# Elementwise work off GpSimd in a planned diffusion-transformer block: subtractions, products and fills on VectorE alone, casts on ScalarE without a handicap

## The chip, the cores and the metric

One NeuronCore of a Trainium2 chip runs the kernel. Its engines work side by side, each through its own queue in order: TensorE (PE in the rows; PEld are its weight loads), VectorE (DVE), ScalarE (ACT), GpSimd (POOL) and SyncE (SP, whose queue SPq issues all DMAs here). The metric is the device time of one execution in microseconds. TensorE's granted clock has two levels, 1.2 and 2.4 GHz; the rows show it as a share of 2.4 GHz.

## The reference

Two layers of a latent diffusion block, on 256 latent tokens and 256 context tokens of width 1024. Cut to what matters:

```
for l in range(DEPTH):                                # DEPTH = 2
    mod_x = silu(c) @ w_ada[l] + b_ada[l]             # shift, scale, gate; the same for the context
    hx = rms_norm(x, norm_w[l]) * (1 + scale_x) + shift_x
    px = split(hx @ w_in[l], SPLIT_POINTS)            # q, k, v and gate columns of four mixers
    ...
    qa = rope(rms_norm(px[0]) * gain)                 # all q and k: norm, gain, and rope in A, C, D
    y_a = window_sink_attention(...)                  # B: 2-D neighbourhood, C: dense, D: differential
    ...
    branches = [y_a * silu(px[3]), y_b * silu(px[7]), y_c * silu(px[11]), y_d * silu(px[15])]
    x_new = x + gate_x * (sum_n(sigmoid(g_n) * (branches[n] @ w_br[l, n])) @ w_out[l])
    if l < DEPTH - 1:                                 # the context stream too, in the first layer
        ctx = ...
```

All matrices are float32, and the result is wanted near float32 precision.

## The kernel before

Every large product is made of three matmuls in the fp32r format (`mm3`): an operand is split into a high part, which is the value cast to fp32r, and a low part, the value less its high part. So each weight block `raw` that a DMA brings becomes `wh` (a cast, by ScalarE or VectorE, list `AV`) and `wl` (a subtraction, by VectorE or GpSimd, list `VG`), in `split_ops`. The normalized, modulated input becomes `hT` in an upper half `hh` (a cast) and a lower half `hl` (a subtraction) in `modulate`. The other instructions of list `VG` are the products of q and k with gains, rope tables and inverse norms (tiles `qk`, `ru`, `st`), the bias with its mask, the zeroes beside mixer B's scores, y times its gate, the merge of the four branches (`merged`) and the sums into the residual.

The start is special. Shift and scale (`mods`) of layer 0 come out of 16 units of w_ada, two for each k tile of 128 rows. A unit is made on VectorE (`ada_unit`: two long products with a sum each), on TensorE (`ada_unit_pe`) or by GpSimd and ScalarE (`ada_unit_pool`: GpSimd makes two products of 1024 columns, tiles `t4k` and `V`, and ScalarE sums each). The string `ADA` says which; five units are GpSimd's, and neither version touches that. The first two groups of projections go k tile by k tile behind the units: `mods`, then `t2k` = x * scale + shift, then `hh`, then `hl`, then the matmuls into `ppj`, `psc` and `ptr` that read hT.

The program is first recorded: each call becomes an operation with the engines that may run it, its cost on each and its dependencies (`alt`, `cost`). Then a planner (`schedule`) puts the operations in an order, engine by engine, by a list-scheduling pass over a model of the engines; an operation of several engines goes to the one where it would end first, with `BIAS` added in the comparison. `search` repeats the pass six times with the operations ordered by their latest start and keeps the best. The instructions are then issued in that order, and each engine keeps it. `ready` holds the model's rule that some instructions of VectorE and GpSimd exclude each other (`port`). All instructions go through one helper, so that every row of the profile has the line L271, and tiles tell them apart.

Of the kernel before, what the change touches and what calls it, by code (L numbers as in the profile page):

```python
# [93 lines left out]
TAIL = 2  # L94
HOLD = 12
WARM = 9
AV, VG = ("scalar", "vector"), ("vector", "gpsimd")
BIAS = {"vector": 0.55, "gpsimd": 0.0, "scalar": 0.35}
ENGS = ("tensor", "scalar", "vector", "gpsimd", "sync")
DMA_FIX, DMA_RATE, LOOK = (0.63, 0.93), 360e3, 60  # L100
GATE = 4096 / 1200.0
# [72 lines left out]
class Recorder:  # L174
# [143 lines left out]
    def schedule(self):  # L318
        ops = self.ops
        for o in ops:  # L320
            o.need, o.fin, o.users = len(o.deps), None, []
        for o in ops:
            for d in o.deps:
                ops[d].users.append(o.i)

        first, left = {}, {}
        for name, a in self.acc.items():
            first[name] = min(o.i for o, _, _ in a)
            left[name] = len({o.i for o, _, _ in a})
        fifo, free, index, kind = {}, {}, {}, {}  # L330
        for name in sorted(first, key=first.get):
            tag, bufs = self.tag[name]
            g = GROUP.get(tag, tag)
            kind[name] = g, tag
            q = fifo.setdefault(tag, [])
            index[name] = len(q)
            q.append(name)
            free.setdefault(g, [(0.0, k) for k in range(bufs if g == tag else BANKS)])
        ptr, held = dict.fromkeys(fifo, 0), dict.fromkeys(fifo, 0)
        shared = {g: [d for d in SURE if GROUP[d] == g] for g in set(GROUP.values())}  # L340
        got, since, tend, taken = {}, {}, {}, []
        bank = {}
        avail = {e: [] for e in ENGS}

        def slot_time(o):

            t, used = 0.0, {}
            for name in o.tiles:
                if name in got:
                    t = max(t, since[name])  # L350
                    continue
                g, tag = kind[name]
                k = used.get(tag, 0)
                room = len(free[g])
                if g in shared:
                    room = min(room, max(SURE[tag] - held[tag],
                                         room - sum(max(0, SURE[d] - held[d]) for d in shared[g] if d != tag)))
                ahead = index[name] - ptr[tag] - k
                if room <= k + (RESERVE.get(tag, 99) if ahead > 0 else 0) or ahead > WINDOW:
                    return None  # L360
                t = max(t, sorted(free[g])[k][0])
                used[tag] = k + 1
            return t

        port = dict.fromkeys(ENGS, 0.0)

        def ready(o, e, s):
            r = max(o.at[e], s)
            if o.port[e]:
                r = max(r, port["gpsimd" if e == "vector" else "vector"])  # L370
            for name in o.banks:
                for f, x in bank.get(name, {}).items():
                    if f != e:
                        r = max(r, x + LAT[f, e])
            return r

        def release(o):
            for e in o.ways:
                bisect.insort(avail[e], (o.prio, o.i))
                o.at[e] = max([0.0, o.hold] + [ops[d].fin + LAT[ops[d].eng, e] for d in o.deps])  # L380

        for o in ops:
            o.at = {}
            o.hold = o.late - HOLD if "sync" in o.ways and not o.raw else 0.0
            if o.need == 0:
                release(o)
        t_free = dict.fromkeys(ENGS, 0.0)
        t_free["sync"] = 0.55
        dma_free, order = 0.0, []
        queue = deque(o.i for o in ops if o.raw)  # L390
        work, gate, slow = {}, 0, True
        while len(order) < len(ops):
            best = None
            for e in ENGS:
                tf, c = t_free[e], None
                if best is not None and tf >= best[0]:
                    continue
                for prio, i in (avail[e][:LOOK] if e != "sync" else avail[e]):
                    if ops[i].raw and i != queue[0]:
                        continue  # L400
                    s = slot_time(ops[i])
                    if s is None:
                        continue
                    o = ops[i]
                    s = s + 0.15 if s else 0.0
                    r = ready(o, e, s)
                    if len(o.ways) > 1:
                        mine = max(r, tf) + o.costs[e] + BIAS[e]
                        if any(max(ready(o, f, s), t_free[f]) + o.costs[f] + BIAS[f] < mine
                               for f in o.ways if f != e):  # L410
                            continue
                    if r <= tf:
                        c = (tf, e, i)
                        break
                    if c is None or r < c[0]:
                        c = (r, e, i)
                if c is not None and (best is None or c[0] < best[0]):
                    best = c
            if best is None:
                raise RuntimeError("no instruction can be scheduled")  # L420
            t, e, i = best
            o = ops[i]
            for f in o.ways:
                avail[f].remove((o.prio, i))
            o.eng = e
            if o.raw:
                queue.popleft()
            order.append(i)
            for name in o.tiles:
                if name not in got:  # L430
                    g, tag = kind[name]
                    z = min(free[g])
                    free[g].remove(z)
                    since[name], got[name] = z
                    held[tag] += 1
                    taken.append(name)
                    q = fifo[tag]
                    while ptr[tag] < len(q) and q[ptr[tag]] in got:
                        ptr[tag] += 1
            c = o.costs[e]  # L440
            if e == "tensor":
                while gate < int(t / GATE):
                    slow = work.get(gate, 0.0) < (0.6 if slow else 0.38) * GATE
                    gate += 1
                c *= 1 + slow
                for k in range(gate, int((t + c) / GATE) + 1):
                    work[k] = work.get(k, 0.0) + min(t + c, (k + 1) * GATE) - max(t, k * GATE)
            o.fin = t_free[e] = t + c
            if o.port[e]:
                port[e] = o.fin  # L450
            if o.dma:
                dma_free = max(dma_free, o.fin + DMA_FIX[0]) + o.dma / DMA_RATE
                o.fin = dma_free + DMA_FIX[1]
            o.start = t
            for name in o.banks:
                bank.setdefault(name, {})[e] = o.fin
            for name in o.tiles:
                left[name] -= 1
                tend[name] = max(tend.get(name, 0.0), o.fin)
                if left[name] == 0:  # L460
                    g, tag = kind[name]
                    free[g].append((tend[name], got[name]))
                    held[tag] -= 1
            for u in o.users:
                q = ops[u]
                q.need -= 1
                if q.need == 0:
                    release(q)
        self.makespan = max(o.fin for o in ops)
        self.got, self.taken, self.kind, self.order = got, taken, kind, order  # L470
# [1311 lines left out]
```

## Time and profile before

| | |
|---|---|
| median of three runs | 1323.66 us (1319.93 to 1325.12) |
| the profiled execution | 1319.68 us |
| its span, first to last instruction | 1317.9 us |
| TensorE busy | 1243.6 us, 94% |
| VectorE busy | 1003.8 us, 76% |
| ScalarE busy | 757.1 us, 57% |
| GpSimd busy | 626.9 us, 48% |

The profile is of one execution. A line of a group gives an engine, an operation, the tiles that it writes and reads, the shapes and the count, then busy time and mean duration, then the time that the engine sat idle before it and what ended that. A busy engine is one whose instruction is under way, which includes an instruction that waits inside its engine for a resource.

### The profile page before, as it was taken

How to read it: one execution, taken by the hardware profiler on the slowest of the kernel's cores; microseconds unless marked ns; L12 is line 12 of the kernel's file. 1: busy time of each engine (PE TensorE's matmuls, PEld its weight loads, DVE VectorE, ACT ScalarE, POOL GpSimd, SP SyncE). 2: the span in 40 equal slices, each digit the busy share in tenths (PEclk: the TensorE clock that was granted, in tenths of full speed). 3: DMA queues.
4: the chain of work that ended last, by engine and by line, in shares of the span. 5: the costliest groups of instructions: out<-in, count | busy, mean ns of one | idle time of the engine just before them, and what ended most of it. 6: DMA issues, size and time to landing. Idle time of an engine off the chain costs nothing. (4 is left out here: it accounts for less than half of the span.)

```text
span 1317.9 us, 21363 instructions
## 1 busy us (share of the span) xinstructions
PE 1243.6 (94%) x7286; PEld 1083.4 (82%) x7286; DVE 1003.8 (76%) x2074; ACT 757.1 (57%) x1761; POOL 626.9 (48%) x705
## 2 busy tenths in 40 slices
PE   7379999999999999999999999889999899999998
PEld 5267888888988989888887888788899899998997
DVE  7858983992889587995878667788794767897876
ACT  5356862473775336653555445577784657665663
POOL 4557311623654535512444003474866577574632
PEclk8689999999999999999999999999999899999999
DMA  6532122522343353333322247342434544343554
GB/s 241 159 116 71 49 90 86 160 64 67 103 108 116 108 151 94 91 114 123 115 81 65 80 153 256 94 137 73 152 109 120 177 143 152 122 144 97 155 167 174
DMA packets 64576, 160.90 MB, mean 122 GB/s; under 512 B 13482, under 2 KB 24914, under 8 KB 64468
## 3 DMA queue, kind: packets, MB, share of 16 engines
q1 hardware_dynamic: 64468, 159.55, 39.3%
q8 instruction: 57, 0.93, 0.3%
q14 instruction: 51, 0.42, 0.1%
HBM read 157.42 MB, written 5.88 MB: 124 GB/s over the span
## 5 line engine op out<-in xcount | busy, mean ns | idle before, releaser
L271 PE MATMUL ppj<-wh,hT 128*128 128x512 f32 (+2 forms) x1424 | 387.4, 350 | 34.6 <-ACT hT L271 34.2
L271 ACT ACTIVATE wh<-raw 128x512 fp32r<-128x512 f32 (+2 forms) x432 | 254.6, 603 | 270.5 <-PE ppj L271 196.7
L271 POOL TENSOR_TENSOR wl<-raw,wh 128x512 fp32r<-128x512 f32 (+2 forms) x190 | 221.1, 1172 | 311.6 <-PE ppj L271 164.3
L271 PE MATMUL ppj<-hT,wh 128*128 128x512 f32 (+1 forms) x1408 | 363.3, 342 | 0.0
L271 PEld LDWEIGHTS ppj<-wh,hT 128*128 128x128 f32 x1424 | 253.0, 191 | 60.2 <-ACT hT L271 35.1
L271 DVE TENSOR_TENSOR wl<-raw,wh 128x512 fp32r<-128x512 f32 (+1 forms) x290 | 210.7, 739 | 86.7 <-PE ppj L271 59.7
L271 PEld LDWEIGHTS ppj<-hT,wh 128*128 128x128 f32 x1408 | 241.4, 189 | 26.8 <-PE ppj L271 0.2
L271 PE MATMUL ppj<-wl,hT 128*128 128x512 f32 (+2 forms) x712 | 247.8, 350 | 1.6 <-POOL wl L271 1.6
L271 PE MATMUL ppj<-hT,wl 128*128 128x512 f32 (+1 forms) x704 | 241.1, 343 | 0.4 <-DVE wl L271 0.3
L271 ACT ACTIVATE P<-psc,st 128x512 f32<-128x512 f32 (+2 forms) x192 | 114.7, 601 | 58.8 <-DVE st L271 53.4
L271 PEld LDWEIGHTS ppj<-wl,hT 128*128 128x128 f32 x712 | 136.1, 192 | 13.9 <-POOL wl L271 2.2
L271 PEld LDWEIGHTS ppj<-hT,wl 128*128 128x128 f32 x704 | 133.0, 189 | 14.7 <-DVE wl L271 0.7
L271 PE MATMUL ppj<-yT,wh 128*128 128x512 f32 (+1 forms) x512 | 130.2, 339 | 0.3 <-ACT yT L271 0.3
L271 DVE TENSOR_REDUCE st<-psc 128x1 f32<-128x512 f32 (+2 forms) x160 | 101.2, 661 | 0.8
L271 PE MATMUL psc<-K,Q 128*128 128x512 f32 (+2 forms) x384 | 95.3, 357 | 5.6 <-ACT P L271 2.0
L271 PE MATMUL ptr<-ident,P 128*128 128x128 f32 x560 | 89.7, 277 | 11.5 <-DVE P L271 6.1
L271 POOL TENSOR_TENSOR st<-st,expo 128x8 f32<-128x8 f32 (+3 forms) x68 | 96.2, 1418 | 3.6
L271 PEld LDWEIGHTS ppj<-yT,wh 128*128 128x128 f32 x512 | 87.1, 188 | 10.8 <-ACT yT L271 0.5
L271 PEld LDWEIGHTS ptr<-ident,P 128*128 128x128 f32 x560 | 67.2, 142 | 27.6 <-ACT P L271 8.4
L271 POOL TENSOR_TENSOR ru<-qk,rtab 128x256 f32<-128x256 f32 (+1 forms) x34 | 25.0, 735 | 134.8 <-ACT qk L271 134.1
L271 PE MATMUL ppj<-yT,wl 128*128 128x512 f32 (+1 forms) x256 | 86.6, 339 | 0.0
L271 DVE TENSOR_REDUCE st<-t2k 128x4 f32<-128x256 f32 (+3 forms) x114 | 42.0, 381 | 53.7 <-ACT t2k L271 51.2
(174 smaller groups left out, 2124.7 us busy)
## 6 DMA issues: line engine op xcount, KB each, us to landing
raw<-in_w_G SPq DMA_DIRECT2D x64, 512.0 KB
raw<-in_w_ada SPq DMA_DIRECT2D x43, 512.0 KB
raw<-in_w_br SPq DMA_DIRECT2D x32, 512.0 KB
raw<-in_w_in_D SPq DMA_DIRECT2D x32, 512.0 KB
raw<-in_w_S SPq DMA_DIRECT2D x24, 512.0 KB
raw<-in_w_in_B SPq DMA_DIRECT2D x32, 384.0 KB
raw<-in_w_out SPq DMA_DIRECT2D x24, 512.0 KB
raw<-in_w_in_A SPq DMA_DIRECT2D x8, 512.0 KB
```

Of the source, the lines that this page charges most:

```text
L271: getattr(getattr(self.nc, eng), fn)(*args, **kw)
```

## The change

`VG` now holds VectorE alone, so that no operation of that list may go to GpSimd, and ScalarE has no handicap when an operation of list `AV` is placed. Three edits of the planner go with it: of engines that could start at the same time, the one whose instruction could have asked earlier is taken (`asked` is `ready` without the port's rule); an engine that is free at the same time as the best one so far is looked at too; and the first candidate that could start at once is compared with those before it. GpSimd keeps the rsqrt steps, the rope table and the products of `ada_unit_pool`.

```
-AV, VG = ("scalar", "vector"), ("vector", "gpsimd")
-BIAS = {"vector": 0.55, "gpsimd": 0.0, "scalar": 0.35}
+AV, VG = ("scalar", "vector"), ("vector",)
+BIAS = {"vector": 0.55, "gpsimd": 0.0, "scalar": 0.0}
...
-        def ready(o, e, s):
+        def asked(o, e, s):
+
             r = max(o.at[e], s)
-            if o.port[e]:
-                r = max(r, port["gpsimd" if e == "vector" else "vector"])
             for name in o.banks:
                 for f, x in bank.get(name, {}).items():
                     if f != e:
                         r = max(r, x + LAT[f, e])
             return r
+
+        def ready(o, e, s):
+            r = asked(o, e, s)
+            return max(r, port["gpsimd" if e == "vector" else "vector"]) if o.port[e] else r
...
-                if best is not None and tf >= best[0]:
+                if best is not None and tf > best[0]:
                     continue
...
+                    if c is None or r < c[0]:
+                        c = (max(r, tf), max(tf, asked(o, e, s)), e, i)
                     if r <= tf:
-                        c = (tf, e, i)
                         break
-                    if c is None or r < c[0]:
-                        c = (r, e, i)
-                if c is not None and (best is None or c[0] < best[0]):
+                if c is not None and (best is None or c[:2] < best[:2]):
                     best = c
...
-            t, e, i = best
+            t, _, e, i = best
```

The whole order is planned anew. On GpSimd, in the start, the rows before were these, where `V` and `t4k` are the products of `ada_unit_pool` (a new number is a new unit) and `wl` the low parts of the second group's weights:

```order
L271 TENSOR_TENSOR t4k<-V_92,scb 128x1024
L271 TENSOR_TENSOR V_92<-V_92,scb 128x1024
L271 TENSOR_TENSOR wl<-raw,wh 128x256 x2
L271 TENSOR_TENSOR t4k<-V_127,scb 128x1024
L271 TENSOR_TENSOR V_127<-V_127,scb 128x1024
L271 TENSOR_TENSOR t4k<-V_162,scb 128x1024
L271 TENSOR_TENSOR V_162<-V_162,scb 128x1024
```

The same place of GpSimd's queue now, up to the third unit:

```order
L271 TENSOR_TENSOR t4k<-V_103,scb 128x1024
L271 TENSOR_TENSOR V_103<-V_103,scb 128x1024
L271 TENSOR_TENSOR t4k<-V_123,scb 128x1024
L271 TENSOR_TENSOR V_123<-V_123,scb 128x1024
L271 TENSOR_TENSOR t4k<-V_165,scb 128x1024
L271 TENSOR_TENSOR V_165<-V_165,scb 128x1024
```

The two wl between the first and the second unit are gone from GpSimd, and so are all later ones: its ten products now follow each other.

VectorE's queue in the start, before, from the second chunk's weights to the lower half of k tile 2's hT (the last row). `raw,scb` are the long products of `ada_unit`, and the last row but one is the scale of k tile 2, made from the second unit of GpSimd:

```order
L271 TENSOR_SCALAR t2k<-merged,mods_125 128x256
L271 TENSOR_TENSOR wl<-raw,wh 128x512
L271 TENSOR_TENSOR hT<-t2k,hT 128x512
L271 SCALAR_TENSOR_TENSOR t2k,st<-raw,scb 128x1024 x2
L271 SCALAR_TENSOR_TENSOR raw,st<-raw,scb 128x1024 x2
L271 TENSOR_SCALAR mods_125<-st,bcol,nwc 128x2
L271 TENSOR_SCALAR mods_125<-st,bcol 128x2
L271 TENSOR_SCALAR mods_125<-st,bcol,nwc 128x2
L271 TENSOR_TENSOR hT<-t2k,hT 128x512
```

VectorE's queue now, where the first `mods_118` row is that scale and the last row is the same lower half of k tile 2:

```order
L271 SCALAR_TENSOR_TENSOR raw,st<-raw,scb 128x1024
L271 TENSOR_TENSOR hT<-t2k,hT 128x512
L271 TENSOR_TENSOR wl<-raw,wh 128x256
L271 TENSOR_SCALAR mods_118<-st,bcol,nwc 128x2
L271 TENSOR_SCALAR mods_118<-st,bcol 128x2
L271 SCALAR_TENSOR_TENSOR t2k,st<-raw,scb 128x1024 x2
L271 TENSOR_TENSOR hT<-t2k,hT 128x512
```

The scale and the hT of k tile 2 stand now behind two long products of their own chunk's units; before they stood behind four of the chunk after it and behind k tile 3.

In the second layer, some 930 us into the execution, GpSimd had these rows, which end in products of q and k and a weight's low part:

```order
L271 TENSOR_TENSOR wl<-raw,wh 128x256
L271 TENSOR_TENSOR qk<-qk,st 128x256 x2
L271 TENSOR_TENSOR t2k<-of,gT 128x256
L271 TENSOR_SCALAR st<-st 128x4 x2
L271 TENSOR_TENSOR st<-st,expo 128x4 x2
L271 TENSOR_TENSOR qk<-qk,rtab 128x128
L271 TENSOR_TENSOR qk<-qk,gain 128x128
```

VectorE has them now, between its own softmax and evacuation steps:

```order
L271 TENSOR_TENSOR wl<-raw,wh 128x256 x2
L271 TENSOR_TENSOR V_2361<-ppj,V_2361 128x2x64 x2
L271 TENSOR_TENSOR of<-ptr,t2k 64x256
L271 TENSOR_REDUCE st<-t2k 128x2
L271 TENSOR_TENSOR t2k<-of,gT 128x256
L271 SCALAR_TENSOR_TENSOR t2k,st<-raw,scb 128x1024
L271 TENSOR_TENSOR yT<-t2k,yT 128x256
L271 TENSOR_TENSOR qk<-qk,st 128x128 x2
```

The steps of `VG` stand in one queue with the evacuations of PSUM (`of`, `V_2361`) and the long products of the modulation; the rsqrt steps (`st`) stay behind on GpSimd alone.

## Rows read from the trace of the kernel before

**Rows 1.** The page's busy time, share of the span and instructions of each engine.

```profile
PE 1243.6 (94%) x7286; PEld 1083.4 (82%) x7286; DVE 1003.8 (76%) x2074; ACT 757.1 (57%) x1761; POOL 626.9 (48%) x705
```

**Rows 2.** Stretches of 100 us: busy time by engine, clock, DMA.

```profile
core 0: us, PE busy (x) PEld busy (x) DVE busy (x) ACT busy (x) POOL busy (x), PEclk, DMA share, GB/s
0.00:100.00 100.00, 61.43 (x297) 47.40 (x298) 75.85 (x123) 48.21 (x103) 53.84 (x46) 0.81 0.52 173
100.00:200.00 100.00, 94.94 (x521) 77.33 (x520) 89.95 (x220) 71.38 (x178) 41.08 (x45) 1.00 0.22 69
900.00:1000.00 100.00, 94.98 (x693) 88.24 (x692) 85.26 (x200) 76.27 (x181) 63.08 (x76) 0.98 0.37 111
1000.00:1100.00 100.00, 96.44 (x661) 92.90 (x660) 65.65 (x160) 57.26 (x147) 65.41 (x83) 0.97 0.49 143
```

**Rows 3.** Waits from 0 to 100 us: total, times, longest, in us.

```profile
PE ppj L271 <- ACT hT L271: 34.2, 5, 22.5
POOL wl L271 <- PE ppj L271: 27.3, 4, 11.8
```

**Rows 4.** Timeline of TensorE, 30 to 56 us: start, duration, idle before.

```profile
33.08 0.28 PE L271 MATMUL ppj<-wh,hT 128*128 128x256 f32 x1
55.81 0.79 PE L271 MATMUL ppj<-wh,hT 128*128 128x512 f32 x1 [22.45 <-ACT hT L271]
```

**Rows 5.** Timeline of GpSimd, 16 to 38 us.

```profile
19.02 2.35 POOL L271 TENSOR_TENSOR V<-V,scb 128x1024 f32<-128x1024 f32 x1
25.23 1.82 POOL L271 TENSOR_TENSOR wl<-raw,wh 128x256 fp32r<-128x256 f32 x1 [3.87 <-PE ppj L271]
30.82 0.81 POOL L271 TENSOR_TENSOR wl<-raw,wh 128x256 fp32r<-128x256 f32 x1 [3.77 <-issue]
31.59 3.34 POOL L271 TENSOR_TENSOR t4k<-V,scb 128x1024 f32<-128x1024 f32 x1
```

**Rows 6.** Timeline of SyncE's DMA queue, 15 to 40 us.

```profile
16.55 0.42 SPq L271 DMA_DIRECT2D V<-in_w_ada  x1
```

**Rows 7.** Timeline of ScalarE, 39 to 58 us.

```profile
42.59 1.04 ACT L271 ACTIVATE V<-V 128x1024 f32<-128x1024 f32 x1
...
54.01 1.09 ACT L271 ACTIVATE t2k<-merged,mods 128x256 f32<-128x256 f32 x2 [9.24 <-DVE mods L271]
55.13 0.63 ACT L271 ACTIVATE hT<-t2k 128x512 fp32r<-128x512 f32 x1
```

**Rows 8.** Timeline of VectorE, 21 to 96 us.

```profile
23.31 0.67 DVE L271 TENSOR_TENSOR wl<-raw,wh 128x512 fp32r<-128x512 f32 x1
23.91 1.21 DVE L271 SCALAR_TENSOR_TENSOR t2k<-raw,scb 128x1024 bf16<-128x1024 f32 x1
...
53.70 0.28 DVE L271 TENSOR_SCALAR mods<-st,bcol,nwc 128x2 f32<-128x2 f32 x1
...
89.61 0.89 DVE L271 TENSOR_TENSOR hT<-t2k,hT 128x512 fp32r<-128x512 f32 x1 [1.82 <-ACT hT L271]
```

**Rows 9.** Tile mods, 0 to 100 us: minimum, median and maximum ns.

```profile
L271 DVE TENSOR_SCALAR mods<-st,bcol,nwc x7: 275/289/2372, 25.1 to 77.2; 128x2 f32<-128x2 f32 x7
```

**Rows 10.** Groups of instructions by shape, over the span.

```profile
L271 POOL TENSOR_TENSOR wl<-raw,wh 128x512 fp32r<-128x512 f32 x106 | 140.4, 1329 | 227.2 <-PE ppj L271 110.9 <-ACT wh L271 61.4 <-issue 13.7
L271 DVE TENSOR_TENSOR wl<-raw,wh 128x512 fp32r<-128x512 f32 x278 | 204.5, 748 | 85.8 <-PE ppj L271 58.8 <-ACT wh L271 14.0 <-issue 8.0
L271 DVE TENSOR_TENSOR qk<-qk,st 128x256 f32<-128x256 f32 x20 | 8.0, 419 | 1.9 <-POOL st L271 1.3 <-POOL qk L271 0.6
L271 DVE CAST wh<-raw 128x512 fp32r<-128x512 f32 x40 | 19.6, 494 | 4.7 <-PE ppj L271 2.5 <-POOL wl L271 2.0
```

**Rows 11.** Waits of TensorE from 100 us to the end.

```profile
PE ptr L271 <- DVE P L271: 6.1, 6, 3.3
PE ptr L271 <- DVE Q L271: 4.4, 2, 3.5
PE ptr L271 <- POOL qk L271: 3.4, 3, 2.3
...
PE ppj L271 <- POOL wl L271: 1.6, 2, 1.3
```

## The prediction

> **What bounds the kernel now.** I read the page's busy times first, then stretches of 100 us, then the waits, then the order of single instructions where TensorE stands still.
>
> TensorE is busy for 1243.6 us of a span of 1317.9, VectorE for 1003.8, ScalarE for 757.1 and GpSimd for 626.9 [rows 1]. So TensorE sets the time wherever it is fed, and the time that can be won is where it is not. By stretches that is mainly one place: from 0 to 100 us TensorE is busy for 61.4, against 94 to 96 in the other stretches that I show [rows 2]. Of the 38.6 us that it idles there, 34.2 are waits for ScalarE's hT in five pieces, the longest 22.5 [rows 3]. That piece is seen singly: the last matmul of the first weight chunk starts at 33.08, the next matmul at 55.81 [rows 4]. The granted clock, 0.81 of 2.4 GHz in this stretch and 1.00 in the next [rows 2], says that part of the work around the stops ran at 1.2 GHz.
>
> Why is hT late? Its two halves need shift and scale of k tile 2, and the scale is a unit whose products GpSimd makes. GpSimd's own row says where they stood: a product of the unit before ends at 21.37 (19.02 + 2.35), then two wl subtractions start only at 25.23 and 30.82, held by buffers that TensorE still reads, and the next unit's first product starts at 31.59 [rows 5]. Its weights had been asked for at 16.55 [rows 6]. So about 10.2 us (31.59 - 21.37) were lost in GpSimd's queue behind work that nobody needed yet. In the same 100 us GpSimd's waits of this kind add up to 27.3 us in 4 pieces [rows 3]. A second delay stands in VectorE's queue: ScalarE starts the second sum of that unit at 42.59, but VectorE makes the scale from it only at 53.70, and ScalarE goes on at 54.01 after 9.24 us idle [rows 7, 8].
>
> **What the change does to the start.** The order excerpts show both delays gone: on GpSimd the ten products follow each other with no wl between them, and on VectorE the scale stands ahead of the products of later units.
>
> By the rows: the second unit's products can start at 21.4 and take 2 x 2.35, to 26.1. The last sum on ScalarE, 1.04, to about 27.2. The scale, 0.28; then ScalarE has four t2k instead of two and two hT ahead of it in the new order, 2 x 1.09 + 2 x 0.63, so hT's upper half is there at about 31 instead of 55.76 (55.13 + 0.63) [rows 5, 7, 8]. The lower half is VectorE's, behind two long products of 1.21 whose load I cannot place. I take 35 for both (31 to 38). TensorE ends the first chunk at about 33.4, so the 22.5 us stop nearly goes.
>
> What is late next? VectorE's own work from there to the last hT of the start, counted in the new order: 12 long products x 1.21, 7 wl x 0.67, 6 shorter wl and 5 hT of some 0.4 and 0.7, ten shift and scale of 0.28, 29 us in all [rows 8]. Six GpSimd products remain, 6 x 2.35 = 14.1 us. Do they run beside VectorE? The row of the scale says no: seven of them take 289 ns in the middle and 2372 at most [rows 9], and the longest is the length of a GpSimd product. So the last hT comes between 35 + 29 = 64 (all overlap) and 78 (none does), and loads may add up to 10. I take 77.5, where it now comes at 90.5 (89.61 + 0.89) [rows 8]: **-13 us**, with bounds of -5 (78 and most of the load waits) and -22.
>
> The Trainium skill, SBUF — State Buffer, section Who interferes with whom, says that the port pair which VectorE shares with GpSimd is an exclusive lock: a VectorE instruction with two SBUF inputs and a GpSimd instruction that reads SBUF exclude each other for a whole instruction. The trace agrees in the 2372 ns above; by that rule alone the end would be at 78 and not earlier.
>
> **What moves to VectorE.** Counted in the two orders, 532 instructions leave GpSimd for VectorE: 190 wl, 224 products and sums of qk and rope, 30 merges, 32 fills, 16 biases, 40 others. 201 go from VectorE to ScalarE and 42 the other way. The rsqrt steps, the rope table and the ten products stay.
>
> Prices: a 512-column wl takes 1329 ns on GpSimd and 748 on VectorE, a 256-column qk product 419 on VectorE [rows 10]. 106 x 0.748 plus 84 shorter wl at some 0.5 is 121 us; 161 x 0.42 plus 63 narrow ones at some 0.28, 85; 86 others at some 0.55, 47; the fills, which no row shows on VectorE, between nothing and the 0.28 of the scale's row, 5. Sum 258. Off go 159 casts and scalings net, at some 0.55 (a little above the row of wh at 494, since many are larger or read PSUM), 87. Net +171 us of durations. Rows overlap by about 0.07 (a wl from 23.31 for 0.67, the next at 23.91 [rows 8]): 373 more instructions, -28. And VectorE no longer waits for GpSimd's port: its 278 wl alone average 748 against an undisturbed 670, 22 us; the same share, 12%, on all of VectorE's busy time would be 117. I take 60. So VectorE goes from 1003.8 to about 1087 us, 83% of a span of 1308, still under TensorE's 1243.6. ScalarE gets 159 x some 0.6 = 95, to 65%: no bound, and free of charge under TensorE's work, since ScalarE idles for 43% of the span now. Where that cover fails is the first 30 us, whose four t2k and two hT are in the chain above.
>
> What it costs TensorE after 100 us: its two longest waits for VectorE are 6.1 and 4.4 us, those for GpSimd 3.4 and 1.6 [rows 11]. The 5.0 for GpSimd are to a good part saved, since the same steps take half as long: **-3**. The 10.5 for VectorE grow as its queue does. With busy over idle as the measure, 0.76/0.24 becomes 0.83/0.17, a factor of 1.5, +5; with the smaller VectorE waits not shown, and less for the port, I take **+6**, with bounds of -5 (only the port matters) and +20.
>
> **Sum.** -13 - 3 + 6 = -10, against the profiled execution's own 1319.7 (span 1317.9 and 1.8 around it): 1309.7. The median of the three runs, 1323.7, stands 4.0 above that, so as a median **1313 us**.
>
> **Rivals.**
>
> First, VectorE becomes the bound in the stretches that are tight now (ends slower). From 900 to 1000 us it is busy for 85.3 [rows 2]; GpSimd's 63.1 there cost at most 63.1 x 748/1329 = 35 on VectorE (the few rsqrt in it stay); some 8 of casts and 12% of 85, 10, of port waits go off: 102 of 100. Its present 14.7 idle are waits for others, and if they stay, the stretch grows by 14. From 100 to 200 us the same reckoning on 90.0 and 41.1 gives 94, and +10. From 1000 to 1100 it has room (65.7). Time: 1323.7 - 13 - 3 + 24 = 1332. It decides once VectorE's waits cost TensorE over 22 us more than now. For it: few idle places and one queue in order, where a wl now stands behind softmax steps. Against it: TensorE waited for VectorE for little even at 90% (94.9 busy in that stretch). The Trainium skill, Perfetto Trace Analysis, section Optimizing Scalar/DVE Operations, points this way: where VectorE is saturated, handing work to GpSimd may pay, though it adds that the shared port may undo it. The whole trace has VectorE at 76%, so the rule would bite in these stretches alone.
>
> Second, the start moves its stop instead of losing it: port and loads hold the last hT near 86, -4, and the rest stays +3: 1323. For it: VectorE is busy 75.9 of the first 100 us already.
>
> Third, the port's release shortens VectorE's answers throughout: -22 at the start, -5 for GpSimd's waits, -5 for VectorE's: 1292. For it, the 12% above; against it, those waits are only 10.5 us in the two rows.
>
> **How the numbers follow.** Forecast 0.51, with its own range 1304 to 1322; VectorE bound 0.18; start only moved 0.19; all shortened 0.12. A difference of 0.5%, 6.6 us, is about what can be told from none. Faster (below 1317): 0.45 of the forecast and the third rival, 0.57. Same: 0.06 of the forecast, 0.17 of the second rival and 0.03 of the first, 0.26. Slower (over 1330.3): 0.17. The range 1296 to 1333 leaves out most of the third rival and the upper half of the first, under 2 in 10.
>
> **What would show it.** GpSimd's products follow each other in the first 60 us without a wl; the stop of 22.5 us is under 5; the last hT of the start lies at 72 to 84 us; TensorE's share from 0 to 100 rises to about 75. A 512-column wl on VectorE falls to about 680 ns. VectorE's busy time is 1050 to 1120 us. TensorE's waits for GpSimd after 100 us nearly vanish, those for VectorE grow by less than 15 us. The prediction is wrong if hT is still waited for over 25 us in the start, or if TensorE's busy share from 900 to 1000 falls under 88.

## The result, and the profile after

The changed kernel takes **1300.04 us** in the median of four runs (1299.64 to 1303.3), the kernel before 1323.68 (1319.93 to 1325.12) beside it: a ratio of 0.9831, 95% interval 0.9805 to 0.9857, or 23.6 us faster. Forecast were 1313 us: the direction was right, the gain of 10 us less than half of what came. The profiled execution took 1303.3 us with a span of 1301.5, so the two profiles show 16.4 of the 23.6 us; the rest is that before's profiled execution lay 4.0 us under its median and this one 3.3 over. Of all runs in this document two were slow ones, list_and_bias once at 1528.9 us and the kernel before once at 1381.0; medians leave them out.

The page's busy times of the changed kernel, as in [rows 1]:

```profile
PE 1253.8 (96%) x7286; PEld 1087.8 (84%) x7286; DVE 1079.4 (83%) x2446; ACT 822.4 (63%) x1921; POOL 173.7 (13%) x173
```

VectorE came out as worked out (1087 forecast). ScalarE is busy for 63% and not 65: it gained 65 us where 95 were forecast. The stretches of [rows 2], in the changed kernel:

```profile
core 0: us, PE busy (x) PEld busy (x) DVE busy (x) ACT busy (x) POOL busy (x), PEclk, DMA share, GB/s
0.00:100.00 100.00, 77.15 (x343) 57.75 (x344) 82.08 (x144) 60.50 (x126) 48.67 (x41) 0.90 0.53 179
100.00:200.00 100.00, 99.65 (x539) 81.33 (x538) 87.42 (x222) 78.59 (x192) 3.68 (x4) 1.00 0.25 78
900.00:1000.00 100.00, 97.01 (x716) 91.32 (x717) 88.33 (x220) 73.28 (x176) 11.01 (x12) 1.00 0.40 124
1000.00:1100.00 100.00, 95.08 (x674) 90.80 (x673) 86.89 (x222) 65.35 (x163) 15.20 (x15) 0.97 0.52 159
```

TensorE's share of the first 100 us rises from 61 to 77, at a granted clock of 0.90 of 2.4 GHz instead of 0.81. From 100 to 200 us, where I feared a tight VectorE, it rises from 94.9 to 99.7. Of the four stretches it falls only from 1000 to 1100 us. Among the others the largest fall is from 1100 to 1200 us, 99.2 to 95.9.

The waits of the first 100 us, against [rows 3]:

```profile
POOL t4k L271 <- DMA V<-in_w_ada: 22.7, 4, 11.0
PE ppj L271 <- ACT hT L271: 16.8, 5, 6.1
```

The stop of 22.5 us is gone, though one of 6.1 is left, and the waits for hT are halved. GpSimd now waits for the loads of its units instead of for TensorE. GpSimd's timeline, 19 to 42 us, against [rows 5]:

```profile
19.03 2.38 POOL L271 TENSOR_TENSOR V<-V,scb 128x1024 f32<-128x1024 f32 x1
22.28 2.37 POOL L271 TENSOR_TENSOR t4k<-V,scb 128x1024 f32<-128x1024 f32 x1 [0.87 <-DMA V<-in_w_ada]
24.72 2.71 POOL L271 TENSOR_TENSOR V<-V,scb 128x1024 f32<-128x1024 f32 x1
38.40 2.91 POOL L271 TENSOR_TENSOR t4k<-V,scb 128x1024 f32<-128x1024 f32 x1 [10.96 <-DMA V<-in_w_ada]
```

The second unit starts at 22.28 instead of 31.59. The third starts no earlier than before, where it began at 37.30:

```profile
37.30 2.86 POOL L271 TENSOR_TENSOR t4k<-V,scb 128x1024 f32<-128x1024 f32 x1
```

Its load was asked for only at 32.80, the fifth unit's at 54.61. SyncE's queue issues in order, and in the first 100 us it waits for 41.8 us for VectorE's wl (before 26.0, and 6.1 for GpSimd's). The longest wait for hT that is left, 6.1 us, ends after ScalarE's second sum of that third unit:

```profile
32.80 0.42 SPq L271 DMA_DIRECT2D V<-in_w_ada  x1
...
54.61 0.43 SPq L271 DMA_DIRECT2D V<-in_w_ada  x1
```

```profile
SPq L271 <- DVE wl L271: 41.8, 12, 12.8
```

```profile
44.29 1.06 ACT L271 ACTIVATE V<-V 128x1024 f32<-128x1024 f32 x1 [1.80 <-POOL V L271]
```

```profile
47.14 0.80 PE L271 MATMUL ppj<-wh,hT 128*128 128x512 f32 x1 [6.07 <-ACT hT L271]
```

VectorE's timeline, 22 to 81 us, against [rows 8, 9]:

```profile
22.35 2.84 DVE L271 TENSOR_TENSOR wl<-raw,wh 128x512 fp32r<-128x512 f32 x1
...
34.87 0.68 DVE L271 TENSOR_TENSOR hT<-t2k,hT 128x512 fp32r<-128x512 f32 x1
...
39.00 2.33 DVE L271 TENSOR_SCALAR mods<-st,bcol,nwc 128x2 f32<-128x2 f32 x1
...
80.07 0.69 DVE L271 TENSOR_TENSOR hT<-t2k,hT 128x512 fp32r<-128x512 f32 x1 [2.31 <-ACT hT L271]
```

A wl of 0.67 us lasts 2.84 and a step of 0.28 us 2.33 where they meet the GpSimd products that start at 22.28 and 38.40, so the two engines still exclude each other there. The last hT of the start ends at 80.8 us (before 90.5, forecast 77.5).

Groups by shape over the span, against [rows 10]:

```profile
L271 DVE TENSOR_TENSOR wl<-raw,wh 128x512 fp32r<-128x512 f32 x384 | 262.6, 693 | 71.1 <-PE ppj L271 55.1 <-issue 11.2 <-ACT wh L271 2.9
L271 DVE TENSOR_TENSOR qk<-qk,st 128x256 f32<-128x256 f32 x72 | 28.3, 417 | 6.2 <-POOL st L271 6.0
```

TensorE's waits from 100 us to the end, the eight longest of 14, against [rows 11]:

```profile
PE ptr L271 <- ACT Q L271: 4.2, 3, 2.5
PE ptr L271 <- DVE qk L271: 3.6, 4, 2.2
PE ppj L271 <- ACT th L271: 3.5, 1, 3.5
PE ptr L271 <- DVE t4k L271: 2.0, 4, 0.7
PE ptr L271 <- ACT P L271: 1.3, 4, 0.5
PE psc L271 <- DVE Q L271: 1.1, 3, 0.5
PE ppj L271 <- DVE st L271: 0.7, 1, 0.7
PE psc L271 <- ACT K L271: 0.6, 1, 0.6
```

Summed over all rows of this view by the engine waited for, before: VectorE 19.7, ScalarE 5.7, GpSimd 5.0; after: 8.5, 10.8 and none. The waits for VectorE, which I had growing by 6, fell by 11, though VectorE is busier. All these are numbers of one order each; other orders of both kernels follow below.

### The profile page after: what moved, and what is told of

Read it like the earlier page. It is cut to its first block, busy times and chain, and to the rows that moved or that the text cites. A ratio compares the mean times of both kernels' runs of the same rounds, so it can differ in the third digit from the quotient of the medians.

```text
span 1301.5 us, 21083 instructions
## 1 busy us (share of the span) xinstructions
PE 1253.8 (96%) x7286; PEld 1087.8 (84%) x7286; DVE 1079.4 (83%) x2446; ACT 822.4 (63%) x1921; POOL 173.7 (13%) x173
## 4 chain that ended last, share of the span: by engine, by line
PE 68%; DVE 15%; issue 7%; ACT 6%; POOL 2%; DMA 2%; SPq 0%; DVEq 0%; ACTq 0%; POOLq 0%
PE ppj L271 54%; PE ptr L271 10%; PE psc L271 4%; DVE wl L271 3%; POOL st L271 2%; ACT P L271 2%; DVE st L271 2%; DVE K L271 2%; DVE t2k L271 1%; DVE raw L271 1%; DVE Q L271 1%; ACT wh L271 1%; DVE t4k L271 1%; ACT t2k L271 1%; DVE qk L271 1%
## 5 line engine op out<-in xcount | busy, mean ns | idle before, releaser
L271 ACT ACTIVATE wh<-raw 128x512 fp32r<-128x512 f32 (+2 forms) x455 | 266.9, 603 | 244.6 <-PE ppj L271 182.0
L271 PE MATMUL ppj<-wh,hT 128*128 128x512 f32 (+2 forms) x1424 | 386.7, 350 | 17.4 <-ACT hT L271 16.8
L271 DVE TENSOR_TENSOR wl<-raw,wh 128x512 fp32r<-128x512 f32 (+2 forms) x480 | 312.0, 660 | 97.3 <-PE ppj L271 70.2
L271 POOL TENSOR_SCALAR st<-st 128x8 f32<-128x8 f32 (+3 forms) x68 | 32.3, 475 | 1013.5 <-DVE st L271 877.5
L271 PE MATMUL ppj<-yT,wh 128*128 128x512 f32 (+1 forms) x512 | 133.5, 345 | 4.1 <-ACT th L271 3.5
L271 ACT ACTIVATE P<-P,st 128x512 f32<-128x512 f32 (+2 forms) x152 | 94.2, 642 | 5.7 <-DVE st L271 5.1
L271 POOL TENSOR_TENSOR st<-st,expo 128x8 f32<-128x8 f32 (+3 forms) x68 | 94.9, 1398 | 5.2
L271 PE MATMUL ptr<-t4k,V 128*128 128x256 f32 x480 | 78.2, 288 | 2.5 <-DVE t4k L271 2.0
L271 DVE TENSOR_TENSOR t4k<-ptr,t4k 128x512 fp32r<-128x512 f32 x112 | 76.4, 682 | 4.3 <-ACT t4k L271 3.5
```

Of the source, the lines that this page charges most:

```text
L271: getattr(getattr(self.nc, eng), fn)(*args, **kw)
```

## The experiments

The change has three parts, which the forecast put into one sum: **the list** (`VG` on VectorE alone), **the handicap** (ScalarE's 0.35 set to 0) and **the rules** (the planner's three edits). Eighteen kernels were run, each in turn with the kernel before, whose median beside them was 1321.9 to 1323.3. First, parts apart, and the list by place.

**list_alone.** The kernel before, with

```
-AV, VG = ("scalar", "vector"), ("vector", "gpsimd")
+AV, VG = ("scalar", "vector"), ("vector",)
```

> The kernel before with VG on VectorE alone; the planner's three edits and ScalarE's handicap of 0.35 stay as before. Theory L (the list does it): at least three quarters of the 23.6 us, so 1300 to 1306 us, the first 100 us with TensorE busy for 75 or more, GpSimd's ten products in a row. Rival P (the placing of casts and the tie rules do a good part, since VectorE without ScalarE's help is overloaded): 1310 to 1320, VectorE busy for 1130 us or more, and TensorE's waits for VectorE after 100 us above 20 us.

**others_alone.** The changed kernel with that line as before.

> The changed kernel with VG on VectorE and GpSimd again: only the planner's three edits and ScalarE's lost handicap are left of the change. Theory L: 1318 to 1326 us, the start still with a wait for hT of 15 us or more and wl between GpSimd's products. Rival P: 1305 to 1315.

**start_alone** and **rest_alone.** The changed kernel, with

```
+        if engs is VG and self.first:
+            engs = VS
...
             ps = self.project_first(pre) if l == 0 else {}
+            nc.first = False
```

where `VS` is VectorE alone and `VG` both engines in start_alone, and the reverse in rest_alone.

> The changed kernel, but the list is VectorE alone only for what is recorded up to the end of the first two groups of projections; all later subtractions, products and fills may go to GpSimd as before. If the start is worth about 12 us and the rest 4 to 11, as the progress of TensorE in the two profiles says: 1308 to 1314 us, end of the start as in the changed kernel (last hT near 80), and the curve flat after it. Rival (the whole gain is the start and what follows from it, since an earlier start lets loads and weights run ahead): 1299 to 1304. Rival (the start's gain is given back where GpSimd's queue stands in TensorE's way): above 1316.

> The complement: the list is VectorE and GpSimd in the start as before, VectorE alone after it. If start and rest add up: 23.6 less what the start alone gives, 1308 to 1318 us, with the 20 us stops for hT still in the first 100 us. If the rest is worth nothing or harms (the forecast had +3 for it): 1322 to 1328.

Measured: list_alone 1315.3 us, others_alone 1293.2. So theory L fell at once: in this order the change without the list is faster than with it. Rival P had list_alone's time right, but put others_alone at 1305 or more. The list by place gave 1291.7 (start) and 1303.5 (rest), which fits no sum. The busy times of list_alone, its stretch from 900 to 1000 us and its longest waits of TensorE after 100 us:

```profile
PE 1257.0 (96%) x7286; PEld 1086.4 (83%) x7286; DVE 1120.7 (85%) x2548; ACT 774.5 (59%) x1819; POOL 171.5 (13%) x173
```

```profile
900.00:1000.00 100.00, 95.78 (x686) 88.37 (x685) 97.88 (x250) 78.62 (x191) 8.05 (x8) 0.97 0.37 110
```

```profile
PE ptr L271 <- DVE Q L271: 7.7, 2, 6.8
PE ptr L271 <- DVE qk L271: 3.6, 4, 1.7
```

Even with VectorE busy for 97.9 of 100 us TensorE idles for only 4.2 of them (before 5.0), though it issues 686 matmuls there instead of 693. So a full VectorE is not yet a bound in that stretch. The longest wait, 6.8 us for VectorE's Q, isn't VectorE's work either. TensorE's row at its end, then VectorE's and GpSimd's before it:

```profile
826.43 0.87 PE L271 MATMUL ptr<-ident,Q 128*128 128x128 f32 x3 [6.83 <-DVE Q L271]
```

```profile
825.08 1.20 DVE L271 TENSOR_SCALAR Q<-K,st 128x1024 f32<-128x1024 f32 x1 [5.22 <-POOL st L271]
```

```profile
821.78 0.86 POOL L271 TENSOR_SCALAR gain<-gain 128x256 f32<-128x256 f32 x1 [25.45 <-DMA gain<-in_qk_gain]
822.72 1.40 POOL L271 TENSOR_TENSOR rtab<-gain,t2k 128x256 f32<-128x256 f32 x2
824.20 0.19 POOL L271 TENSOR_SCALAR st<-st 128x1 f32<-128x1 f32 x1
```

VectorE idled for 5.2 us, since the rsqrt step (`st`) stood in GpSimd's queue behind the rope table, whose load came late.

The other four of the eight combinations came next: **bias_alone** is the kernel before with

```
-BIAS = {"vector": 0.55, "gpsimd": 0.0, "scalar": 0.35}
+BIAS = {"vector": 0.55, "gpsimd": 0.0, "scalar": 0.0}
```

**rules_alone** is the kernel before with the planner's edits (`asked`, `tf > best[0]`, the new `c`) alone; **list_and_bias** and **list_and_rules** are the changed kernel without the one or the other.

> The kernel before with ScalarE's handicap of 0.35 set to 0 and nothing else. List and planner's rules are those of before. Three edits without the list gave 1293.2 us. Theory B (the casts do it: ScalarE, idle for 43% of the span, takes some 100 of them, and VectorE's answers come earlier): 1292 to 1300 us, second unit of GpSimd right behind the first, and ScalarE busy for 795 us or more. Theory R (the tie rules do it): 1315 to 1323, with the 22 us stop still there. If the two share it: 1303 to 1312.

> The kernel before with the planner's three edits and nothing else (the list on both engines, ScalarE's handicap 0.35). Theory R: 1292 to 1300 us and the 22 us stop gone. Theory B: 1315 to 1323. If the two share it: 1303 to 1312.

> The changed kernel with the planner's rules of before. With the list alone it was 1315.3 us and with all 1300. Theory B: 1297 to 1303, as the whole change. Theory R: 1311 to 1317. By either the list costs some 7 us against the same kernel with both engines on it.

> The changed kernel with ScalarE's handicap of 0.35 back. Theory R: 1297 to 1303. Theory B: 1311 to 1317, with VectorE at 1110 us or more, since the casts that ScalarE would take stay with it.

Measured: 1300.3, 1308.6, 1306.6 and 1303.2 us. Both B and R hold a part; neither is the whole. bias_alone's busy times, then GpSimd's timeline, 18 to 33 us, and TensorE's at its longest stop:

```profile
PE 1242.1 (96%) x7286; PEld 1079.1 (83%) x7286; DVE 972.6 (75%) x2000; ACT 802.5 (62%) x1871; POOL 584.6 (45%) x669
```

```profile
18.71 2.38 POOL L271 TENSOR_TENSOR V<-V,scb 128x1024 f32<-128x1024 f32 x1
...
29.14 0.75 POOL L271 TENSOR_TENSOR wl<-raw,wh 128x256 fp32r<-128x256 f32 x1 [6.91 <-PE ppj L271]
29.84 3.35 POOL L271 TENSOR_TENSOR t4k<-V,scb 128x1024 f32<-128x1024 f32 x1
```

```profile
57.47 0.79 PE L271 MATMUL ppj<-wh,hT 128*128 128x512 f32 x1 [25.35 <-ACT hT L271]
```

The handicap leaves the stop as it was, with the wl in front of the second unit (29.84); its gain comes after it. The same two places in rules_alone:

```profile
19.56 2.35 POOL L271 TENSOR_TENSOR V<-V,scb 128x1024 f32<-128x1024 f32 x1
...
24.85 1.14 POOL L271 TENSOR_TENSOR wl<-raw,wh 128x256 fp32r<-128x256 f32 x1 [0.72 <-ACT wh L271]
25.94 2.41 POOL L271 TENSOR_TENSOR t4k<-V,scb 128x1024 f32<-128x1024 f32 x1
```

```profile
77.10 0.80 PE L271 MATMUL ppj<-wh,hT 128*128 128x512 f32 x1 [9.58 <-ACT hT L271]
```

Here wl still stand between the units, but short and unheld, and the longest stop is 9.58. So the start is mended in part by the rules without the list, and in part by the list without the rules (its longest wait for hT in list_alone is 13.1).

Each of these kernels also has a wholly new order. How much is that alone? The **replans** change one number of the planner's model that means nothing for the work:

```
-DMA_FIX, DMA_RATE, LOOK = (0.63, 0.93), 360e3, 60
+DMA_FIX, DMA_RATE, LOOK = (0.63, 0.93), 358e3, 60
```

> The kernel before, planned again with one number of the planner's model, DMA_RATE, at 358e3 for 360e3. Nothing else differs, but some two thirds of each queue stand in another order. Theory S (the three parts of the change work by what they move): 1317 to 1327 us, like before. Rival O (the order of before is an unlucky draw, and any new order of it is faster by some 10 us or more): 1300 to 1313 us, the 22 us stop gone.

> The same with DMA_RATE at 362e3. Theory S: 1317 to 1327 us. Rival O: 1300 to 1313 us. One of the two near 1322 and one near 1308 would say that the draw of the order alone is worth 10 us and more, and that no single comparison of this study under that size is settled.

> The changed kernel with DMA_RATE at 358e3. Theory S: 1296 to 1304 us, so that the 7 us that the list costs beside the other edits hold against another order. Rival O: anywhere from 1290 to 1312.

> The three planner's edits and ScalarE's lost handicap without the list, with DMA_RATE at 358e3. Theory S: 1290 to 1297 us, again under the changed kernel's. Rival O: 1290 to 1312, with no fixed place against the changed kernel.

Measured: 1315.0 and 1310.4 us for the kernel before, 1297.4 for the changed one, 1298.7 without the list. Rival O holds for a part: before's own order is the slowest of its three. But the stop stays; in before_replan_a, waits from 0 to 100 us:

```profile
PE ppj L271 <- ACT hT L271: 30.9, 5, 22.7
```

What differs lies in the second layer (the lead after 62.5% of the columns in the table below is 1.0 and -2.5 us, at the end 4.4 and 9.3). And the list's 7 us beside the other parts did not hold: in the second draw the changed kernel is 1.2 us ahead.

The last six: the list in one layer only, in two draws each (`nc.first = not last` at the head of the layer loop sets the place), and a second draw of the handicap and of the rules.

> The changed kernel with the list on VectorE alone in the first layer only; in the second layer GpSimd may take its part again. Planner's edits and ScalarE's lost handicap stay. Theory X (the list gains some 4 us in the first layer and costs some 6 in the second, where VectorE is then busy for 86 to 98 of 100 us and TensorE waits for it): 1288 to 1295 us, the progress curve some 15 to 19 us ahead of before at 750 us and not falling back later. Rival Y (the differences between these kernels are the draw of the order): 1292 to 1303 and no fixed place against the next run.

> The complement: the list on VectorE alone in the second layer only. Theory X: 1300 to 1307 us, and the curve falls back by 5 us or more between 750 us and the end. Rival Y: 1292 to 1303.

> The list in the first layer only, planned with DMA_RATE at 358e3. Theory X: 1288 to 1296 us. Rival Y: 1292 to 1303, and 5 us or more from the other draw.

> The list in the second layer only, planned with DMA_RATE at 358e3. Theory X: 1299 to 1307 us, above both kernels with the list in the first layer. Rival Y: 1292 to 1303, and under one of them.

> ScalarE's handicap at 0 alone (list and rules of before), planned with DMA_RATE at 358e3. The three orders of before gave 1322, 1315 and 1310 us, 1316 in the mean; the first draw of this kernel 1300.3. If the casts on ScalarE are worth some 10 us in any order: 1299 to 1309 us, TensorE's waits for VectorE after 100 us under 12 us (before has 19.7, 15.2 and 9.6), the stop for hT in the start still there. Rival (the draw): 1310 to 1318.

> The planner's three edits alone, planned with DMA_RATE at 358e3; the first draw gave 1308.6 us. If they are worth some 8 us in any order, by the start: 1301 to 1311 us, and TensorE's waits for hT in the first 100 us at 17 to 25 us against 31 to 34 in the three orders of before. Rival (the draw): 1311 to 1320, waits for hT near 31.

Measured: 1294.3 and 1298.5 us with the list in the first layer, 1297.2 and 1298.0 in the second, bias_replan 1304.1, rules_replan 1300.4. Theory X fell: the list's place makes no difference that stands out from the draw. Handicap and rules held in the second draw.

All kernels together, before with the mean of its medians. Waits are TensorE's, in us: for ScalarE's hT from 0 to 100 us, all from 100 us to the end, and those of them for VectorE. The lead is worked out from the rows of the matmuls: how much earlier than before the kernel had started 62.5% and 100% of all matmul columns.

| kernel | us | ratio, 95% interval | hT | later | VectorE | lead 62.5%, end |
|---|---|---|---|---|---|---|
| before | 1322.7 | | 34.2 | 30.4 | 19.7 | 0, 0 |
| before_replan_a | 1315.0 | 0.9932-0.9960 | 30.9 | 28.8 | 15.2 | 1.0, 4.4 |
| before_replan_b | 1310.4 | 0.9898-0.9926 | 31.4 | 19.6 | 9.6 | -2.5, 9.3 |
| list_alone | 1315.3 | 0.9924-0.9963 | 20.9 | 24.3 | 19.5 | 9.7, 1.6 |
| bias_alone | 1300.3 | 0.9808-0.9845 | 31.6 | 15.7 | 8.0 | 11.0, 19.4 |
| bias_replan | 1304.1 | 0.9848-0.9893 | 29.1 | 16.6 | 7.5 | 7.5, 15.6 |
| list_and_bias | 1306.6 | 0.9869-0.9908 | 20.8 | 18.8 | 11.2 | 11.7, 12.8 |
| rules_alone | 1308.6 | 0.9879-0.9908 | 22.8 | 23.1 | 11.9 | 8.9, 11.0 |
| rules_replan | 1300.4 | 0.9820-0.9860 | 20.9 | 23.8 | 12.9 | 16.0, 20.4 |
| list_and_rules | 1303.2 | 0.9839-0.9869 | 10.9 | 21.3 | 12.9 | 14.3, 16.1 |
| others_alone | 1293.2 | 0.9753-0.9797 | 16.9 | 19.2 | 10.3 | 19.8, 24.3 |
| others_replan | 1298.7 | 0.9803-0.9833 | 23.5 | 15.8 | 5.7 | 10.9, 22.4 |
| the changed kernel | 1300.0 | 0.9805-0.9857 | 16.8 | 19.3 | 8.5 | 18.0, 16.0 |
| after_replan | 1297.4 | 0.9790-0.9823 | 12.6 | 16.7 | 7.1 | 19.3, 24.5 |
| start_alone | 1291.7 | 0.9747-0.9791 | 12.6 | 14.3 | 5.2 | 17.0, 29.4 |
| rest_alone | 1303.5 | 0.9836-0.9879 | 20.7 | 22.5 | 6.2 | 11.4, 15.5 |
| layer1_list | 1294.3 | 0.9768-0.9802 | 18.8 | 17.0 | 8.6 | 18.3, 24.4 |
| layer2_list | 1297.2 | 0.9790-0.9823 | 23.9 | 15.5 | 6.7 | 12.0, 22.4 |
| layer1_list_replan | 1298.5 | 0.9793-0.9830 | 19.7 | 18.5 | 4.1 | 15.6, 20.9 |
| layer2_list_replan | 1298.0 | 0.9797-0.9833 | 24.9 | 16.1 | 7.1 | 10.2, 21.3 |

Means of the medians by handicap and rules, whatever the list: neither 1315.8 (4 kernels), handicap 1303.7 (3), rules 1304.1 (3), both 1297.3 (10). Within these groups the kernels scatter by 3.9 us (pooled standard deviation): that is the draw, with what the list and its place may add, and the standard errors below come from it. The handicap gives 12.1 without the rules and 6.8 with them, **9.5 us, standard error 2.0**; the rules 11.8 and 6.4, **9.1, error 2.0**. The list, from the four pairs of means without and with it (1316.0 and 1315.3; 1302.2 and 1306.6; 1304.5 and 1303.2; 1295.9 and 1298.7), **costs 1.3, error 2.2**: nothing that can be told. Before's own order is 6.7 us slower than the mean of its three (1316.0). 9.5 + 9.1 + 6.7 - 1.3 = 24.0, of the 23.6 us measured; the same medians go into both, so this shares the gain out and does not prove the shares.

start_alone, 1291.7 us, others_alone, 1293.2, and layer1_list, 1294.3, beat both kernels with intervals that lie under the changed kernel's. Since kernels that differ from them in nothing but the order or the list's place lie at 1297.2 to 1303.5, I count them as good draws and not as better ideas.

## Why the prediction was wrong in size

**What bounds the kernel** held: TensorE, and the start as its largest idle place.

**The start, -13**, held: the stop went, the last hT came within the forecast's 72 to 84 us, and TensorE had started the first 5% of its columns 11.3 us earlier than before. That it comes at 80.8 and not at 77.5 is in line with what now stands in GpSimd's row, loads: 22.7 us in four waits, where I had allowed for 10; the third and fifth were asked for late. The second unit itself came as worked out: VectorE's half of its hT ended at 35.55 (forecast 35). But I named one cause, the wl that leave GpSimd. The runs show two, and either takes off a third: old rules with both engines wait 29 to 34 us for hT in five draws, the list alone 20.8 and 20.9, the rules alone 20.9 and 22.8, list and rules together 10.9 to 19.7 in the six kernels with the list in the whole first layer or the start. Which of the rules' three edits does it was not tried apart.

Two readings there don't hold: rows 5 put the second wl's 3.77 us of idling down to issue, not to TensorE's buffers, and VectorE's 29 us add up to 27.9.

**The waits for GpSimd, -3**, were -5.0 against this order of before; its replans had 1.5 and 0.7 us of them.

**The waits for VectorE, +6**, is the step that failed: "With busy over idle as the measure, 0.76/0.24 becomes 0.83/0.17, a factor of 1.5". They went from 19.7 to 8.5 us, the wrong sign; in the mean of the draws, from 14.8 (three) to 7.8 (two). VectorE's busy time says little of how long TensorE waits for it: list_alone has VectorE at 1120.7 us and waits of 19.5, the same as before at 1003.8, and 6.8 of them come from GpSimd's queue; bias_alone takes 31 us off it and has 8.0. What decides it in general no run shows; which instructions stand ahead of the needed one in a queue is my reading of single rows. I costed the casts that go to ScalarE as durations only, "free of charge". They are the half of the change that works after the stop: without the new rules, TensorE's later waits are 17.0 us in the mean of the three kernels whose handicap is gone against 25.8 in the four that have it, and the three are 12.1 us faster (9.5 in the mean with and without the rules). The Trainium skill, Perfetto Trace Analysis, section Optimizing Scalar/DVE Operations, says that such a handover to ScalarE may make sense where VectorE is saturated; here it paid at 76%. What it says beside that, that handing work between VectorE and GpSimd might not help, the runs agree with (1.3 us, error 2.2).

Against these gains stand 5.1 us more of waits for ScalarE (5.7 to 10.8), which I had at nothing; before's replans had 12.2 and 9.3, so they may be the draw. All waits behind the start fell by 11.1 us (30.4 to 19.3), but the lead grew by only 4.7 there (11.3 to 16.0), while TensorE was busy for 10.2 us more over the span (see Open, below).

**Profile and median.** I added 4.0 us because before's profiled execution lay that much under its median; the changed kernel's lies 3.3 above its own. That is 7.3 of the 13.7 us between the sum (1313.7) and the result. The other 6.4 are the sum against the changed kernel's profiled 1303.3: by the leads, 1.7 too much for the start, and some 8 too little behind it.

**Not in the forecast at all** was the draw of the order. In the mean of the draws the change is worth 1316.0 - 1298.7 = 17.3 us, error 3.5; 6.7 came from the order that before happened to have.

**The rivals.** The first, VectorE as the bound, fell: its 102 of 100 us from 900 to 1000 came out as 88.3, and list_alone's 97.9 cost TensorE little there. The second, a moved stop, did not happen. The third, the port's release, came nearest to the sign of the waits, but not by its cause: where both engines share the list a 512-column wl on VectorE takes 743 to 773 ns, with the list on VectorE 687 to 693, and that 7 to 13% moved no time that can be told. others_alone has the slow wl and is the faster kernel:

```profile
L271 DVE TENSOR_TENSOR wl<-raw,wh 128x512 fp32r<-128x512 f32 x286 | 214.1, 756 | 87.4 <-PE ppj L271 68.4 <-issue 7.1 <-ACT wh L271 5.1
```

**Open** stays why the list loses what it wins in the start, where it cuts the waits for hT by 5 to 11 us. By the table's leads it loses it after 62.5% of the columns, in the second layer: the five kernels with the list everywhere lose 0.4 us against before there in the mean, the eight without it, before left out, gain 6.8. But the two layer2_list kernels, which have the list in that layer, gain 10.4 and 11.1, so its being there is not enough. One trace of it: in the five kernels with the list everywhere TensorE is busy for 1248.2 to 1257.0 us, in the nine without it for 1242.1 to 1250.0, 7.0 more in the mean, with the same 7286 matmuls. No run tells what these are.

## What to carry to other kernels

When a planner writes the order, one kernel before and one after measure the change and the draw together: replan each with a number that means nothing, two or three times, before a difference under some 10 us is put down to an edit. Cost each edit apart, the one-number ones too: here the edit that moved 532 instructions was worth nothing that can be told, and 0.35 us in a table some 9 us. And don't scale an in-order engine's waits by its busy share; follow the longest ones back singly, since a wait put down to VectorE can stand in GpSimd's queue.

## What I had not expected of the hardware

In list_alone VectorE was busy for 97.9% of a stretch of 100 us with TensorE at 95.8%, so there an in-order engine near full hardly held up the one that it feeds. And medians of one order agree far better than orders: the kernel before gave 1321.9 to 1323.3 us in five series of runs, while its three orders span 12 us.
